# Row-wise dot products with a softmax: who sums step 6, where the last loads of x are cut, and who sets the ones

## The chip, the cores and the metric

The kernel runs on one core of one Trainium2 chip. The metric is the device time of one execution in microseconds; a lower number is better. The times shown are medians of several executions, and beside them stands one execution that was profiled: its instructions and DMA packets come from the trace.

## The reference

```
def reference(x, y):                      # x, y: 8 x 4096 x 512, float32
    gram = np.matmul(x, y.transpose(0, 2, 1))
    diag = np.diagonal(gram, axis1=1, axis2=2)
    diag = diag - diag.max(axis=-1, keepdims=True)
    exp = np.exp(diag)
    return (exp / exp.sum(axis=-1, keepdims=True)).astype(np.float32)
```

Only the diagonal of each product is used, so what must be computed is, for each of 8 x 4096 rows, the dot product of a row of x with the same row of y (512 elements), and then a softmax over the 4096 dot products of each of the 8 batches. Each input is 67 MB and is read once.

## The kernel before

**Layout.** Four batches (Q) stand on the 128 partitions at a time, 32 partitions (G) a batch, so each partition holds 128 rows (C) of one batch. The two halves of the batches make 2 x 128 rows a partition. The work goes in S = 8 steps of R = 32 rows a partition: steps 0 to 3 give the first four batches, 4 to 7 the last four. A step's x is 128 x 16384 floats, 8 MB, and so is its y. x has two buffers (`xs0`, `xs1`, taken by step number modulo 2), y has one (`ys`). The dot products of a half are the columns of `diag0` and `diag1`; step 6 gives columns 64 to 95 of `diag1`, step 7 columns 96 to 127.

**Order.** The schedule is written out by hand: each engine runs its instructions in the order of the program, and an instruction waits only for the data and the buffers that it needs. All loads go out on one queue, SP's, and are worked off in that order.

**Steps 0 to 5** (the first loop of the main part). SP loads 32 rows of x and 32 of y. ScalarE copies the last 6 rows of y aside (`side`), VectorE multiplies x by y in place (`products`, L76), the rows of 26 first and then the 6 from `side`, so that `ys` comes free for the next load before the last product. Then VectorE sums 30 rows with one reduction (`sums`, L79) and ScalarE two rows with one instruction a row (`sums_act`, L84: a copy with an accumulated sum, and an accumulator read). After step 3 the softmax of the first half runs (`exps`, `normalize`).

**Step 6.** The loads are the same. ScalarE copies rows 8 to 16 of y (9 rows) to the unused end of the other x buffer, L146. VectorE multiplies rows 0 to 7, then 8 to 16 from the copy, then 17 to 31. The first of these frees rows 0 to 16 of `ys` for step 7, the last one frees the rest. ScalarE then sums rows 0 to 29, VectorE rows 30 and 31, and VectorE takes the maximum of columns 0 to 63 of `diag1` into a spare column, C + 1 (`largest`, L104).

**Step 7.** GpSimd sets 16 columns behind `ys` to 1 (L156; the program order puts it here, it waits for nothing and runs at the start). SP's loads come in pieces: x in 15, 8, 6, 2 1/2 and 1/2 rows, y in 17, 9, 3 and three times 1. Between the loads the program lists the dot products whose x and y are both in by then. Each row is one VectorE instruction with an accumulated sum (`dot`, L87), shown in the profile as SCALAR_TENSOR_TENSOR and DVE_READ_ACCUMULATOR. When 17 rows are done, VectorE takes the maximum of columns 64 to 111 into column C.

Row 31 is split into two dots, as its x comes in two pieces. The first writes its sum into the column of the x buffer just behind row 31 (`chained`). The second is one column longer than its piece: it takes in that sum, times the 1 that stands behind `ys`. Thus it waits for the last load of x (L182), for the first part's accumulator and for the ones.

**The end.** ScalarE copies columns 0 to 95 of `diag1` (L186). The first half's result is stored by SP in six pieces. Then VectorE takes the maximum over columns 112 to 129, over the partitions of a batch, ScalarE makes the exponentials and their sums, VectorE the sum over the partitions, its reciprocal and the product, and ScalarE's queue stores the last half's result (L191).

The lines that set the cuts, before:

```
    for load, n in (
        (load_x, H - 1), (load_y, F), (load_x, 8), (load_y, 9), (load_x, 6), (load_y, 3), (load_y, 1)
    ):                                   # H = 16, F = 17
        load(t, upto[load], n)
        upto[load] += n
        both = min(upto.values())
        dots(t, done, both - done)
        done = both
```

Of the kernel before, what the change touches and what calls it, by code (L numbers as in the profile page):

```python
# [11 lines left out]
def kernel(  # L12
# [6 lines left out]
    nc = tc.nc  # L19
# [5 lines left out]
    B, N, D = x.shape  # L25
# [3 lines left out]
    C = N // G  # L29
    R = 32  # L30
    H = R // 2
    K = 6
    W = 2
    F = H + 1
    L = 9
    E = 16
    V = D // 2
    S = B // Q * (C // R)


# [9 lines left out]
    yflat = big.tile([P, R * D + E], f32, name="ys")  # L50
# [4 lines left out]
    diag = [small.tile([P, C + 2 * i], f32, name=f"diag{i}") for i in range(B // Q)]  # L55
# [6 lines left out]
    def rows(t, r0, n):  # L62
        return xs[t % 2][:, r0 : r0 + n, :]

    def dots_of(t, r0, n):
        return diag[t * R // C][:, columns(t, r0, n)]
# [4 lines left out]
    def load_y(t, r0, n):  # L71
        nc.sync.dma_start(out=ys[:, r0 : r0 + n, :], in_=yv[t * R // C, :, columns(t, r0, n), :])

    def products(t, r0, n, yt):
        xt = rows(t, r0, n)
        nc.vector.tensor_tensor(out=xt, in0=xt, in1=yt, op=Alu.mult)  # L76

    def sums(t, r0, n):
        nc.vector.tensor_reduce(out=dots_of(t, r0, n), in_=rows(t, r0, n), axis=X, op=Alu.add)  # L79

    def sums_act(t, r0, n):
        for r in range(r0, r0 + n):
            row = xs[t % 2][:, r, :]
            nc.scalar.activation(out=row, in_=row, func=Act.Copy, accum_out=dots_of(t, r, 1))  # L84

    def dot(xt, yt, out):
        nc.vector.scalar_tensor_tensor(  # L87
            out=xt, in0=xt, scalar=1.0, in1=yt, op0=Alu.mult, op1=Alu.mult, accum_out=out
        )

    def dots(t, r0, n):
        for r in range(r0, r0 + n):
            dot(xs[t % 2][:, r, :], ys[:, r, :], dots_of(t, r, 1))

    def over_quadrant(name, column, op, negate=False):

        got = small.tile([P, 1], f32, name=name)
        nc.vector.tensor_reduce(  # L98
            out=got, in_=column.to_broadcast([P, G]), axis=X, op=op, negate=negate, apply_transpose=True
        )  # L100
        return got

    def largest(out, d):
        nc.vector.tensor_reduce(out=out, in_=d, axis=X, op=Alu.max)  # L104

    def exps(i, d):
        mxp = small.tile([P, 1], f32, name=f"mxp{i}")
        largest(mxp, d)
        nmx = over_quadrant(f"nmx{i}", mxp, Alu.max, negate=True)
        sump = small.tile([P, 1], f32, name=f"sump{i}")  # L110
        nc.scalar.activation(out=res[i], in_=diag[i][:, :C], func=Act.Exp, bias=nmx, scale=1.0, accum_out=sump)  # L111
        return sump

    def normalize(i, sump):
        total = over_quadrant(f"sum{i}", sump, Alu.add)
        rc = small.tile([P, 1], f32, name=f"rc{i}")
        nc.vector.reciprocal(out=rc, in_=total)  # L117
        nc.vector.tensor_single_scalar(out=res[i], in_=res[i], scalar=rc, op=Alu.mult)  # L118
# [4 lines left out]
    nc.vector.addr_align(128, offset=0, max_nops=0)  # L123
    nc.scalar.addr_align(128, offset=0, max_nops=0)

    nc.sync.drain()
    nc.sync.drain()

# [13 lines left out]
    t = S - 2  # L142
# [4 lines left out]
    products(t, 0, F - L, ys[:, : F - L, :])  # L147
    products(t, F - L, L, spare)
    products(t, F, R - F, ys[:, F:, :])
    sums(t, R - W, W)  # L150
    sums_act(t, 0, R - W)
    largest(diag[1][:, C + 1 :], diag[1][:, : C - 2 * R])


    t += 1
    nc.gpsimd.memset(yflat[:, R * D :], 1.0)  # L156
    chained = xflat[t % 2][:, R * D : R * D + 1]
    late = R * D - V
    upto = {load_x: 0, load_y: 0}
    done = 0  # L160
    for load, n in (
        (load_x, H - 1), (load_y, F), (load_x, 8), (load_y, 9), (load_x, 6), (load_y, 3), (load_y, 1)
    ):
        load(t, upto[load], n)
        upto[load] += n
        both = min(upto.values())
        dots(t, done, both - done)
        done = both
        if done == F:
            largest(diag[1][:, C : C + 1], diag[1][:, C - 2 * R : C - R + H])  # L170

    first = (R - 3) * D
    xt = xflat[t % 2]
    xrow = xv[t * R // C].rearrange("p c d -> p (c d)")
    end = ((t % (C // R)) + 1) * R * D
    nc.sync.dma_start(out=xt[:, first : late], in_=xrow[:, end - R * D + first : end - V])
    dots(t, done, 1)
    load_y(t, R - 2, 1)
    dots(t, R - 2, 1)
    load_y(t, R - 1, 1)  # L180
    dot(xt[:, late - V : late], yflat[:, late - V : late], chained)
    nc.sync.dma_start(out=xt[:, late : R * D], in_=xrow[:, end - V : end])  # L182
    dot(xt[:, late : R * D + 1], yflat[:, late : R * D + 1], dots_of(t, R - 1, 1))

# [2 lines left out]

    for p, n in ((0, H), (H, H), (2 * H, H), (3 * H, H), (4 * H, 2 * H), (6 * H, 2 * H)):
        nc.sync.dma_start(out=ov[0, p : p + n, :], in_=res[0][p : p + n, :])
    normalize(1, exps(1, diag[1][:, C - R + H :]))  # L190
    nc.scalar.dma_start(out=ov[1], in_=res[1])  # L191


# [28 lines left out]
```

## Time and profile before

| | |
|---|---|
| median of 3 runs | 319.77 us (319.74 to 320.01) |
| profiled execution | 319.84 us |
| its span, first to last instruction | 318.1 us |
| VectorE busy | 241.6 us, 76% of the span, 100 instructions |
| ScalarE busy | 49.8 us, 16%, 97 instructions |
| GpSimd busy | 0.3 us, 5 instructions |
| read from HBM | 134.22 MB, 422 GB/s over the span |
| VectorE's products (L76) | 96.7 us in 8 instructions of the long form, 20.1 in 6 of the short one |
| VectorE's sums (L79) | 98.1 us in 7 instructions |
| VectorE's dots of step 7 (L87) | 20.0 us in 33 instructions |
| ScalarE's sums (L84) | 25.9 us in 42 instructions |

How to read it: DVE in the profile is VectorE, ACT is ScalarE, POOL is GpSimd, SP is SyncE, which only issues DMAs here. A "q" behind an engine's name is its sequencer. The span is counted from the first instruction, and all times in the timeline are us from there. L87 is line 87 of the kernel, and where a helper records an operation, it is the helper's line. In the timeline the columns are the start, the length, the engine, the line, the operation, out<-in with shapes, and in brackets the idle time before it with what ended that. A line of the DMA issues has the size of the load in KB and the us from its issue to its landing.

### The profile page before, as it was taken

How to read it: one execution, taken by the hardware profiler on the slowest of the kernel's cores; microseconds unless marked ns; L12 is line 12 of the kernel's file. 1: busy time of each engine (PE TensorE's matmuls, PEld its weight loads, DVE VectorE, ACT ScalarE, POOL GpSimd, SP SyncE). 2: the span in 40 equal slices, each digit the busy share in tenths (PEclk: the TensorE clock that was granted, in tenths of full speed). 3: DMA queues.
4: the chain of work that ended last, by engine and by line, in shares of the span. 5: the costliest groups of instructions: out<-in, count | busy, mean ns of one | idle time of the engine just before them, and what ended most of it. 6: DMA issues, size and time to landing. Idle time of an engine off the chain costs nothing. (4 is left out here: it accounts for less than half of the span.)

```text
span 318.1 us, 320 instructions
## 1 busy us (share of the span) xinstructions
DVE 241.6 (76%) x100; ACT 49.8 (16%) x97; POOL 0.3 (0%) x5
## 2 busy tenths in 40 slices
DVE  0000069995899939999399994999939998599995
ACT  1000030100301003010020103101030100596700
POOL 0000000000000000000000000000000000000000
DMA  9999999999999999999999999999999999999993
GB/s 373 420 396 478 445 396 437 486 396 396 478 445 396 453 470 396 396 478 445 396 470 453 396 396 486 437 396 478 445 396 404 519 396 396 441 435 399 449 405 129
DMA packets 3971, 134.37 MB, mean 422 GB/s; under 512 B 513, under 2 KB 897, under 8 KB 1537
## 3 DMA queue, kind: packets, MB, share of 16 engines
q1 hardware_dynamic: 3824, 134.29, 97.9%
q10 hardware_dynamic: 144, 0.07, 0.1%
q14 instruction: 3, 0.02, 0.0%
HBM read 134.22 MB, written 0.13 MB: 422 GB/s over the span
## 5 line engine op out<-in xcount | busy, mean ns | idle before, releaser
L76 DVE TENSOR_TENSOR xs<-xs,ys 128x13312 f32<-128x13312 f32 (+2 forms) x8 | 96.7, 12091 | 71.4 <-DMA ys<-in_y_dram 71.4
L79 DVE TENSOR_REDUCE diag<-xs 128x30 f32<-128x15360 f32 (+1 forms) x7 | 98.1, 14020 | 0.2
L84 ACT ACTIVATE xs<-xs 128x512 f32<-128x512 f32 x42 | 25.9, 616 | 90.4 <-DVE xs L76 90.4
L132 ACT ACTIVATE side<-ys 128x3072 f32<-128x3072 f32 x6 | 16.6, 2763 | 124.0 <-DMA ys<-in_y_dram 124.0
L87 DVE SCALAR_TENSOR_TENSOR xs<-xs,ys 128x512 f32<-128x512 f32 (+2 forms) x33 | 20.0, 673 | 0.8 <-DMA ys<-in_y_dram 0.6
L76 DVE TENSOR_TENSOR xs<-xs,side 128x3072 f32<-128x3072 f32 x6 | 20.1, 3351 | 0.0
L84 ACT ACTIVATION_READ_ACCUMULATOR xs<-xs 128x1 f32 x42 | 7.8, 186 | 0.0
L146 ACT ACTIVATE xs<-ys 128x4608 f32<-128x4608 f32 x1 | 4.0, 4043 | 20.0 <-DMA ys<-in_y_dram 20.0
L111 ACT ACTIVATE res<-diag,nmx 128x128 f32<-128x128 f32 x2 | 0.8, 401 | 29.9 <-DVE nmx L98 29.9
L76 DVE TENSOR_TENSOR xs<-xs,xs 128x4608 f32<-128x4608 f32 x1 | 5.0, 4951 | 0.0
L87 DVE DVE_READ_ACCUMULATOR xs<-xs,ys 128x1 f32 x33 | 2.8, 84 | 0.0
L122 ACT ACT_TABLE_LOAD x1 | 1.3, 1283 | 0.7 <-PEq L206 0.7
L98 DVE TRANSPOSE_TENSOR_REDUCE sum<-sump 128x1 f32<-128x32 f32 x2 | 0.4, 211 | 1.2 <-ACT res L111 1.2
L118 DVE TENSOR_SCALAR res<-res,rc 128x128 f32<-128x128 f32 x2 | 0.6, 286 | 0.1
L104 DVE TENSOR_REDUCE mxp<-diag 128x1 f32<-128x128 f32 (+1 forms) x2 | 0.5, 229 | 0.1
L98 DVE TRANSPOSE_TENSOR_REDUCE nmx<-mxp 128x1 f32<-128x32 f32 x2 | 0.4, 212 | 0.1
L104 DVE TENSOR_REDUCE diag<-diag 128x1 f32<-128x64 f32 (+1 forms) x2 | 0.4, 204 | 0.0
L117 DVE RECIPROCAL rc<-sum 128x1 f32<-128x1 f32 x2 | 0.3, 164 | 0.1
L111 ACT ACTIVATION_READ_ACCUMULATOR res<-diag,nmx 128x1 f32 x2 | 0.4, 186 | 0.0
L186 ACT ACTIVATE met<-diag 128x96 f32<-128x96 f32 x1 | 0.3, 283 | 0.0
L156 POOL MEMSET ys<- 128x16 f32 x1 | 0.1, 111 | 0.3 <-POOLq L206 0.3
L206 POOL MEMSET const-bfloat16-1.0<- 128x1 bf16 x1 | 0.1, 101 | 0.0
(3 smaller groups left out, 0.3 us busy)
## 6 DMA issues: line engine op xcount, KB each, us to landing
ys<-in_y_dram SPq DMA_DIRECT2D x1, 4352.0 KB, 14.8
xs<-in_x_dram SPq DMA_DIRECT2D x1, 3840.0 KB, 14.2
ys<-in_y_dram SPq DMA_DIRECT2D x1, 2304.0 KB, 12.2
xs<-in_x_dram SPq DMA_DIRECT2D x1, 2048.0 KB, 19.3
xs<-in_x_dram SPq DMA_DIRECT2D x1, 1536.0 KB, 15.6
ys<-in_y_dram SPq DMA_DIRECT2D x1, 768.0 KB, 16.9
ys<-in_y_dram SPq DMA_DIRECT2D x3, 256.0 KB, 18.3
xs<-in_x_dram SPq DMA_DIRECT2D x1, 640.0 KB, 18.2
```

The costliest lines, as they stand in the source:

```text
L76: nc.vector.tensor_tensor(out=xt, in0=xt, in1=yt, op=Alu.mult)
L79: nc.vector.tensor_reduce(out=dots_of(t, r0, n), in_=rows(t, r0, n), axis=X, op=Alu.add)
L84: nc.scalar.activation(out=row, in_=row, func=Act.Copy, accum_out=dots_of(t, r, 1))
L87: nc.vector.scalar_tensor_tensor(out=xt, in0=xt, scalar=1.0, in1=yt, op0=Alu.mult, op1=Alu.mult, accum_out=out)
L98: nc.vector.tensor_reduce(out=got, in_=column.to_broadcast([P, G]), axis=X, op=op, negate=negate, apply_transpose=True)
L104: nc.vector.tensor_reduce(out=out, in_=d, axis=X, op=Alu.max)
L111: nc.scalar.activation(out=res[i], in_=diag[i][:, :C], func=Act.Exp, bias=nmx, scale=1.0, accum_out=sump)
L117: nc.vector.reciprocal(out=rc, in_=total)
L118: nc.vector.tensor_single_scalar(out=res[i], in_=res[i], scalar=rc, op=Alu.mult)
L122: nc.scalar.preload_act_table(Act.Exp)
L132: nc.scalar.activation(out=side, in_=ys[:, R - K :, :], func=Act.Copy)
L146: nc.scalar.activation(out=spare, in_=ys[:, F - L : F, :], func=Act.Copy)
```

## The change

- Step 6: ScalarE sums all 32 rows. VectorE's sum of rows 30 and 31 and its maximum of columns 0 to 63 go.
- Step 7: x comes in 12, 11, 6, 2 3/8 and 5/8 rows in place of 15, 8, 6, 2 1/2 and 1/2. Row 31 is cut after 192 columns in place of 256 and its second part has 320. The loads of y and the order of all loads stay.
- The maximum behind row 16 of step 7 now spans columns 0 to 111 in place of 64 to 111. The last maximum spans columns 112 to 128 (17 values) in place of 112 to 129.
- The ones: VectorE sets one column ahead of step 0, in place of GpSimd's 16 columns.

```diff
-    V = D // 2
+    V = 5 * D // 8
+    U = D - V
...
+    nc.vector.memset(yflat[:, R * D : R * D + 1], 1.0)
+
     nc.sync.drain()
     nc.sync.drain()
...
-    sums(t, R - W, W)
-    sums_act(t, 0, R - W)
-    largest(diag[1][:, C + 1 :], diag[1][:, : C - 2 * R])
+    sums_act(t, 0, R)
...
-    nc.gpsimd.memset(yflat[:, R * D :], 1.0)
...
-        (load_x, H - 1), (load_y, F), (load_x, 8), (load_y, 9), (load_x, 6), (load_y, 3), (load_y, 1)
+        (load_x, R - L - 11), (load_y, F), (load_x, 11), (load_y, 9), (load_x, 6), (load_y, 3), (load_y, 1)
...
-            largest(diag[1][:, C : C + 1], diag[1][:, C - 2 * R : C - R + H])
+            largest(diag[1][:, C : C + 1], diag[1][:, : C - R + H])
...
-    dot(xt[:, late - V : late], yflat[:, late - V : late], chained)
+    dot(xt[:, late - U : late], yflat[:, late - U : late], chained)
...
-    normalize(1, exps(1, diag[1][:, C - R + H :]))
+    normalize(1, exps(1, diag[1][:, C - R + H : C + 1]))
```

## The prediction

> **What bounds the kernel now.** I read the page first, then SP's timeline with the landing times of its loads, then VectorE's timeline of the last step, each for what ends last.
>
> ```profile
> DVE 241.6 (76%) x100; ACT 49.8 (16%) x97; POOL 0.3 (0%) x5
> ...
> DMA  9999999999999999999999999999999999999993
> ...
> HBM read 134.22 MB, written 0.13 MB: 422 GB/s over the span
> ```
>
> The reader is to see that no engine is full, but that the 16 DMA engines are, in every slice but the last. All of the input passes once through them. So the first question about any edit is whether it moves the moment at which the last byte lands.
>
> SP's timeline of the last loads (start, length, engine, line), and then the size and the time from issue to landing of five of them, from the DMA view:
>
> ```profile
> 269.10 0.33 SPq L69 DMA_DIRECT2D xs<-in_x_dram  x1
> 278.74 0.33 SPq L72 DMA_DIRECT2D ys<-in_y_dram  x1
> 279.12 0.43 SPq L69 DMA_DIRECT2D xs<-in_x_dram  x1
> 291.64 0.33 SPq L72 DMA_DIRECT2D ys<-in_y_dram  x1
> ...
> 293.44 0.43 SPq L176 DMA_DIRECT2D xs<-in_x_dram  x1
> ...
> 298.46 0.33 SPq L182 DMA_DIRECT2D xs<-in_x_dram  x1
> ```
>
> ```profile
> ys<-in_y_dram SPq DMA_DIRECT2D x1, 4352.0 KB, 14.8
> xs<-in_x_dram SPq DMA_DIRECT2D x1, 3840.0 KB, 14.2
> ...
> xs<-in_x_dram SPq DMA_DIRECT2D x1, 2048.0 KB, 19.3
> ...
> xs<-in_x_dram SPq DMA_DIRECT2D x1, 640.0 KB, 18.2
> xs<-in_x_dram SPq DMA_DIRECT2D x1, 128.0 KB, 14.7
> ```
>
> Issue plus landing time gives the order in which data comes in: x rows 0 to 14 at 283.3, y rows 0 to 16 at 293.5, x rows 15 to 22 at 298.4, and at the end x row 29 to half of row 31 at 311.6 and the last half row at 313.2. Eight rows of 256 KB take 298.4 - 293.5 = 4.9 us, so a row takes 0.61 us, in one unbroken line: each load is issued 3 us or more before the one ahead of it is through. The last byte lands at 313.2.
>
> VectorE beside it:
>
> ```profile
> 291.65 1.22 DVE L79 TENSOR_REDUCE diag<-xs 128x2 f32<-128x1024 f32 x1
> 292.79 0.21 DVE L104 TENSOR_REDUCE diag<-diag 128x1 f32<-128x64 f32 x1
> 293.63 0.69 DVE L87 SCALAR_TENSOR_TENSOR xs<-xs,ys 128x512 f32<-128x512 f32 x1 [0.64 <-DMA ys<-in_y_dram]
> ...
> 311.70 0.69 DVE L87 SCALAR_TENSOR_TENSOR xs<-xs,ys 128x512 f32<-128x512 f32 x1
> ...
> 312.93 0.42 DVE L87 SCALAR_TENSOR_TENSOR xs<-xs,ys 128x256 f32<-128x256 f32 x1
> 313.27 0.08 DVE L87 DVE_READ_ACCUMULATOR xs<-xs,ys 128x1 f32 x1
> 313.45 0.43 DVE L87 SCALAR_TENSOR_TENSOR xs<-xs,ys 128x257 f32<-128x257 f32 x1
> ```
>
> From 293.63 on it works without a pause: 32 rows, one each 0.61 us. It reaches row 29 at about 311.6, just when that row's x lands (311.6), so in the last 2 us VectorE and the loads are level. Only the last dot is behind its data: x is there at 313.2, it starts at 313.45. Behind it comes a fixed tail (largest, exp, sum, division, store) of 318.1 - 313.45 = 4.6 us.
>
> **The sums of step 6.** Off VectorE go the sum of two rows (1.22 us at 291.65) and the maximum over 64 (0.21 at 292.79), some 1.3 us in all, ahead of the first dot. They do not set that dot: it waits a further 0.64 us for y, which lands at 293.5. Taken alone this edit is worth nothing at the end. ScalarE gets two more rows at 0.61 us (its own pitch: 298.40, 299.01). It now does 15 rows from 291.65 on instead of 13, so it ends near 300.9 instead of 299.6; its next need is the exp at 314.4, which leaves 13 us of cover. The moved maximum grows from 48 to 112 columns (0.20 us for 48, 0.21 for 64: I take 0.2) and gets a new wait on ScalarE's last sum. Queued behind it on VectorE are all dots from row 17 on. It is reached at 302.3 (below), 1.4 us after ScalarE is through, so the wait costs nothing; were ScalarE later, a further 1.6 us of waiting for y would still cover it.
>
> **The cut of x.** The first x load falls from 15 rows to 12, so the y load behind it lands 3 x 0.61 = 1.8 us earlier, at 291.7, with VectorE free at 291.65. Rows 0 to 11 then run from 291.8 to 299.2. The next 11 x rows land at the old 298.4, since as many bytes are ahead of their end (40 rows before and after). Rows 12 to 16 run to 302.2, the maximum to 302.3. Then VectorE must wait for the next y load, issued at 291.64 as before, because it waits for the last product of step 6, which this change does not touch; it takes 12.2 us on the page, so it lands at 303.8. That is 1.5 us of new idle time: the gained start is given back there. From there the loads lead: x rows 23 to 28 land at 307.6 (292.01 + 15.6), the next y at 309.4 (292.49 + 16.9), and rows 26 to 28 end at 311.3, before x row 29 comes.
>
> **The last two pieces.** The larger one loses 64 columns (32 KB, 0.08 us), so it lands near 311.55 and row 29 starts at 311.62; rows 30 and 31 follow each 0.61 later, row 31's first part at 312.85, with their y 0.08 us earlier too. A dot of 512 columns takes 0.61 to its accumulator read and one of 256 takes 0.34 (312.93 to 313.27), so a column costs 1.05 ns and 192 columns take 0.27: accumulator read at 313.12. The last dot needs that value; the old distance from read to start is 0.18, giving 313.30. Its x lands at the old 313.2, since the total of bytes ahead is the same, and 0.09 us from landing to start (293.54 to 293.63) gives 313.25 to 313.29. I take 313.30, 0.15 earlier than now. It is then 64 columns longer: 0.07. Net **-0.08 us**. The maximum of 17 in place of 18 values and the rest of the tail stay.
>
> **The ones.** GpSimd's set (0.11 us at 0.73) goes and VectorE sets one column at about 0.8 us, where it is idle for 42 us until step 0's data lands; no load touches that column. If that cover were gone it would cost about the 0.1 of GpSimd's row. The last dot then has one engine less to wait for, which could shorten its 0.18 us by at most the 0.09 that lies between the end of the accumulator read and the dot's start; the landing at 313.2 lets it keep none to 0.05 of it. I take 0.
>
> **Sum.** The profiled execution is 319.84 (span 318.1 and 1.7 around it), so 319.84 - 0.08 = 319.76; it lies 0.07 above the median of 319.77, so the median becomes 319.69: **319.7 us**. A difference under 0.2% (0.64 us) is what a measurement here can't tell from none, so this is no change.
>
> **The price that this trace does not show: the start of the y load.** The y load at 278.74 can only go out once step 6's first product is done. Today x ahead of it covers its start. The DMA view, in slices of 25 ns from 281.9:
>
> ```profile
> DMA  0000000909909009900009000000000090999000
> ...
> DMA packets 32, 0.56 MB, mean 557 GB/s; under 512 B 16, under 2 KB 16, under 8 KB 16
> ```
>
> These are the 16 engines' first packets of y, at 282.1 to 282.8, 3.3 to 4.1 us after issue. With three x rows less the engines are free at 280.2 to 281.0, 1.5 to 2.2 us after issue. How long an issued load needs to start is shown once: the first load of the program goes out at 0.83, and its packets start at 1.85 to 2.85, 1.0 to 2.0 us later. If the same engine is last both times, nothing is lost; in the opposite order an engine would lose 2.0 - 1.5 = 0.5 us. From above the loss is bounded by the cover that has been enough so far, 3.3 us: at most 3.3 - 1.5 = 1.8. From below by 0, since an earlier start of y is already counted. I take 0, by the start row, the nearest.
>
> The Trainium skill, DMA: Bandwidth & Descriptors, section "Latency and other measured facts", puts the first byte of a load issued by SP at about 0.6 us; by that the cover would be ample and the sum would stay as it is. This trace does not agree: its one uncovered start took 1.0 to 2.0 us, so the risk stays.
>
> **Rivals.** (1) Slower: the y load starts too late, as just worked out. It decides from a start of 1.5 us on, and every tenth goes to the end one for one, because all later loads stand in the same line and the tail hangs on the last. Price 0.1 to 1.8, time 319.8 to 321.5; over the 0.2% only from a start of some 2.2 us on. For it: the uncovered start comes within 0.5 us of that. Against it: that start was the program's first. (2) Faster: VectorE's work, not the loads, sets the end, and 1.8 us of earlier start come through, or most of them: 318.0 to 318.5. For it: 20 us without a pause. Against it: the last x lands at 313.2, and 4.9 us of dot and tail follow; starting with its data, the dot can gain 0.2 at most. It needs loads that end earlier too, as from 302 to 313.2 they run at 391 GB/s against 432 from 23 to 302; at the full rate 11.2 us would be 10.1, so 1.1 us faster, 318.7. Nothing in the change raises that rate. (3) The sums don't fit: ScalarE is slower beside VectorE's dots than its 0.61 and the maximum waits. It needs 3 us of delay to be felt; before, ScalarE held its pitch beside the dots.
>
> **Chances.** Forecast, with a small start loss included: 0.83. Rival 1 above 0.2%: 0.09. Rival 2: 0.06. Rival 3: 0.02, half of it past 0.2%. So faster 0.06, same 0.84, slower 0.10. The range takes the forecast with the spread of the runs before (319.74 to 320.01), a gain of 0.3 more and the 0.5 us of a late start: 319.3 to 320.2.
>
> **What would show it.** Right: first dot at about 291.8, an idle gap of about 1.5 us on VectorE waiting for y after row 16, row 29 waiting for x near 311.55, last x landed at 313.2, last dot at 313.3. The late start would show as 16 first packets of y later than 280.2 to 281.0, with every later landing late by as much. VectorE as the bound would show as an end of the chain near 312 with x landed earlier. ScalarE's last sum past 303.9 would prove the third rival.

## The result and the profile after

The changed kernel takes 320.27 us (median of 22 executions, 319.85 to 322.26), the kernel before, on the same chip, 319.96 (22 executions, 319.74 to 320.61). The ratio is 1.0023, 95% interval 1.0012 to 1.0034: slower by a quarter of a percent, where no change was forecast, and the median lies 0.07 us above the forecast range.

The median tells less than the list. Eleven of the 22 executions lie between 319.85 and 320.08, two at 320.47 and 320.66, nine between 321.33 and 322.26, and between 320.66 and 321.33 there is none. So the kernel has two outcomes: in half of the executions it is in the forecast range, with two more a little above it, and in about four of ten it is 1.4 to 2.3 us slower than the kernel before. The profiled execution (322.26, span 320.3) is one of the latter, the slowest of all, which is of use: it shows the loss.

Some 0.15 us of the 0.31 between the medians have nothing to do with the two groups. The time of an execution less its span, the part before the first and after the last instruction, is 1.94 us in the median of the changed kernel (1.87 to 2.03) and 1.79 in the 29 executions of the kernel before that were run beside the first experiments (1.73 to 1.82).

SP's timeline of the last loads, then the same loads in the DMA view (KB, us from issue to landing):

```profile
269.65 0.33 SPq L70 DMA_DIRECT2D xs<-in_x_dram  x1
279.24 0.33 SPq L73 DMA_DIRECT2D ys<-in_y_dram  x1
279.62 0.43 SPq L70 DMA_DIRECT2D xs<-in_x_dram  x1
292.14 0.33 SPq L73 DMA_DIRECT2D ys<-in_y_dram  x1
...
300.71 0.33 SPq L182 DMA_DIRECT2D xs<-in_x_dram  x1
```

```profile
ys<-in_y_dram SPq DMA_DIRECT2D x1, 4352.0 KB, 14.7
xs<-in_x_dram SPq DMA_DIRECT2D x1, 3072.0 KB, 12.3
xs<-in_x_dram SPq DMA_DIRECT2D x1, 2816.0 KB, 21.1
...
xs<-in_x_dram SPq DMA_DIRECT2D x1, 160.0 KB, 14.8
```

Everything in this execution is 0.5 us late from the start of step 7 on (the issue at 269.65 against 269.10); that grew in the steps before, which the change hardly touches, and executions of both kernels differ by that much. Add issue and landing time (the second view has the time to the tenth, the landing records give 281.96 and 293.97): 12 rows of x are in at 282.0, y's 17 rows at 294.0. Between these two landings lie 12.0 us; before, for the same 4352 KB, it was 293.54 - 283.28 = 10.26. So **1.75 us are lost in the one load of y**, and nothing after it brings them back: the last x lands at 315.5, 2.3 later than before.

VectorE beside it:

```profile
294.10 0.69 DVE L88 SCALAR_TENSOR_TENSOR xs<-xs,ys 128x512 f32<-128x512 f32 x1 [1.98 <-DMA ys<-in_y_dram]
...
304.51 0.27 DVE L105 TENSOR_REDUCE diag<-diag 128x1 f32<-128x112 f32 x1
306.15 0.69 DVE L88 SCALAR_TENSOR_TENSOR xs<-xs,ys 128x512 f32<-128x512 f32 x1 [1.37 <-DMA ys<-in_y_dram]
...
313.87 0.69 DVE L88 SCALAR_TENSOR_TENSOR xs<-xs,ys 128x512 f32<-128x512 f32 x1 [0.24 <-DMA xs<-in_x_dram]
...
315.58 0.49 DVE L88 SCALAR_TENSOR_TENSOR xs<-xs,ys 128x321 f32<-128x321 f32 x1
```

VectorE now waits three times, each time for a load: it has lost its sums, and it is the loads alone that set the end. The last dot starts 0.09 us after its x has landed (300.71 + 14.8 = 315.5).

Where in y's load the time goes can be seen in the DMA view with a narrow window. The digits are the busy share in 40 slices, placed by the start of each packet; packets under 512 B are the 16 engines' closing writes of the x load, the others first packets of y. First the changed kernel from 280.85 to 282.2, then, for the same 1.35 us from the first such write on, the kernel of the first experiment (15 rows of x ahead, from 281.95):

```profile
DMA  0909990009900900090900900000000000009000
...
DMA packets 31, 0.52 MB, mean 387 GB/s; under 512 B 16, under 2 KB 16, under 8 KB 16
```

```profile
DMA  0099990099900900900099900000900000000000
...
DMA packets 32, 0.56 MB, mean 413 GB/s; under 512 B 16, under 2 KB 16, under 8 KB 16
```

Of 32 packets one is missing in the changed kernel, and one stands alone in slice 37: fourteen engines start y at once, one starts at 282.1, and one still hasn't at 282.2. In the trace's packet records these two start 0.5 and 1.0 us behind the last of the others, at 282.08 and 282.58, though by the packet records both had been through with x since 281.1. Their first packet of 34 KB takes 2.40 and 2.06 us; of the other fourteen, eight take 1.29 and six 1.33 to 1.61. The landings follow: the 16 engines' parts of y's load are in from 291.6 to 294.0, a spread of 2.3 us; before it was 0.8. The trace does not name the engines, but in y's load and in each of the nine loads of x and y behind it two parts of 16 land 1.2 us behind the rest.

The Trainium skill, DMA: Bandwidth & Descriptors, section "Why a DMA increments its semaphore by 16 and not by 1", says that the engines of one DMA finish independently and that only the full count of 16 means that all data are there. The trace agrees: two engines of 16 set the landing of the whole load at 294.0, while half of them had landed by 292.1.

### The profile page after: what moved, and what is told of

It is laid out like the page before. It is cut to its first block, busy times and chain, and to the rows that moved or that the text cites. A ratio compares the mean times of both kernels' runs of the same rounds, so it can differ in the third digit from the quotient of the medians.

```text
span 320.3 us, 321 instructions
## 1 busy us (share of the span) xinstructions
DVE 240.6 (75%) x99; ACT 51.0 (16%) x101; POOL 0.2 (0%) x4
## 4 chain that ended last, share of the span: by engine, by line
DMA 70%; DVE 28%; issue 0%; SPq 0%; ACT 0%; DVEq 0%
DMA ys<-in_y_dram 59%; DVE xs L77 28%; DMA xs<-in_x_dram 11%; DVE xs L88 0%; SPq L73 0%; SPq L70 0%; DVE res L119 0%; DVE sum L99 0%; DVE nmx L99 0%; ACT res L112 0%; DVE mxp L105 0%; DVE rc L118 0%; DVEq L77 0%; DVEq L88 0%; SPq L130 0%
## 5 line engine op out<-in xcount | busy, mean ns | idle before, releaser
L80 DVE TENSOR_REDUCE diag<-xs 128x30 f32<-128x15360 f32 x6 | 96.9, 16153 | 0.2
L85 ACT ACTIVATE xs<-xs 128x512 f32<-128x512 f32 x44 | 27.1, 617 | 90.4 <-DVE xs L77 90.4
```

## The experiments

Theory A: with 12 rows of x ahead of it, y's load is issued too short a time before the DMA engines are free. Single engines begin it late or slowly and lag to the end, which the parts of the later loads bear out. Its rivals: another part of the change (theory B), the load of 12 rows itself, or the load that is issued 0.4 us behind y (A2, against A1, the start of y's own load). The experiments were run on three chips, each beside the kernel before on the same chip.

**The first cut back to 15 and 8 rows, all else changed.**

```diff
-        (load_x, R - L - 11), (load_y, F), (load_x, 11), (load_y, 9), ...
+        (load_x, H - 1), (load_y, F), (load_x, 8), (load_y, 9), ...
```

> The changed kernel with x's first two loads back at 15 and 8 rows; all else of the change stays. Theory A (step 7's first y load starts too late behind 12 rows of x, and single DMA engines then lag to the end): no execution above 320.7, median 319.6 to 320.0, y of 17 rows landing 10.2 to 10.4 us after the x ahead of it. Theory B (the 192 + 320 cut of row 31, the sums on ScalarE or the ones are to blame): part of the executions stay at 321.3 or more, as in the changed kernel.

Measured: 320.01 (11 executions, 319.81 to 320.40), ratio to the kernel before 1.0003 (0.9995 to 1.0012). The upper group is gone, and y's load takes 10.26 us again. The sums on ScalarE, the cut of row 31 and the ones bring nothing that can be measured. They, or one of them, do cost a little outside the span: it is 1.92 us here (1.88 to 2.01), and 1.79 before.

**The first cut alone, in the kernel before.**

```diff
-        (load_x, H - 1), (load_y, F), (load_x, 8), (load_y, 9), ...
+        (load_x, 12), (load_y, F), (load_x, 11), (load_y, 9), ...
```

> The kernel before with only x's first two loads changed to 12 and 11 rows. Theory A: two groups of executions, near 319.9 and 1.4 to 2 us above, at 321.3 to 322.3, some four in ten of them in the upper one. Theory B: all between 319.7 and 320.6 as before.

Measured: 321.02 (12 executions, 319.79 to 322.65), ratio 1.0035 (1.0020 to 1.0050); six of the 12 at 321.19 or more. So the cut alone makes the loss. Two clear groups were expected; here the values in between (320.5 to 320.9) are filled too. In its profile y's load takes 11.6 us. Outside the span it has 1.78 us, as before.

**13 rows, 14 rows, 8 rows** (the changed kernel with 13 and 10, 14 and 9, 8 and 15).

> The changed kernel with 13 and 10 rows. Theory A: 0.6 us more cover for the y load, 2.1 us from its issue to the first free engine; the upper group gets rarer or is gone, median 319.7 to 320.1. Theory B: as the changed kernel, some four executions in ten at 321.3 or more.

> The changed kernel with 14 and 9 rows. Theory A: cover 2.7 us, the upper executions nearly gone, median 319.8 to 320.2, highest below 320.8. With the medians of 15, 13, 12 and 8 rows (320.0, 320.6, 320.3 or 321.0, 322.6) this gives the cost against the cover.

> The changed kernel with 8 and 15 rows: the DMA engines have no x left some 0.2 to 0.9 us before the y load is even issued, so the y load starts from idle queues and its first packets show the bare time from issue to start. Theory A: first packets 1.0 to 2.4 us after issue, every landing behind it later by 2 to 3 us, every execution at 321.8 to 324. Theory B: as the changed kernel, 319.9 or 321.5.

Measured: 13 rows 320.58 (11 executions, 319.83 to 321.26, ratio 1.0020, 1.0010 to 1.0029); 14 rows 320.37 (319.88 to 320.82, 1.0005, 0.9996 to 1.0014); 8 rows 322.56 (322.38 to 322.61, 1.0082, 1.0069 to 1.0095). With more cover the highest values come down: 322.3, 321.3, 320.8, 320.4 for 12, 13, 14 and 15 rows. The last step of these says little: the 320.82 of 14 rows is the profiled execution, in which y's load takes 10.26 us, as before, and step 6's y lands 0.79 us late. The medians were expected 0.5 (13 rows) and 0.2 (14 rows) lower than they are, and that of 13 rows is above that of 12 (320.27).

The kernel with 8 rows shows a bare start. Its y load is issued at 279.14, after the engines have run out of x. The DMA view from 278 to 281, 75 ns a slice:

```profile
DMA  0000500000000000000000000000999009900909
...
DMA packets 32, 0.57 MB, mean 191 GB/s; under 512 B 15, under 2 KB 15, under 8 KB 15
```

By the packet records 15 of the 16 engines are through with x by 278.6 and the last at 279.0, and nothing starts until 280.1. The first packets of y start 1.0 to 1.8 us after issue, and each of these 16 takes 1.62 to 2.16 us, where the next ones take 1.29. So here a start from nothing costs two things, the wait for the first packet and then 0.3 to 0.9 us of slow first packet; together the load of y takes 12.5 us from landing to landing and not 10.26.

**The same bytes ahead, in loads of 12 and 3 rows.**

```diff
-        (load_x, R - L - 11), (load_y, F), (load_x, 11), (load_y, 9), ...
+        (load_x, 12), (load_x, 3), (load_y, F), (load_x, 8), (load_y, 9), ...
```

> The changed kernel, but the 15 rows of x that stood ahead of y before are back as two loads, 12 and 3 rows, and then y's 17 and x's 8. The load of 12 rows stays, the bytes ahead of y are those of before. Theory A (cover of the y load's start by bytes): all executions between 319.7 and 320.5, as with 15 rows in one load. Rival (it is the load of 12 rows itself, its packets or the count of loads): an upper group at 321.2 or more stays.

Measured: 320.10 (11 executions, 319.89 to 320.69), ratio 1.0007 (0.9998 to 1.0016). Nothing above 320.7, though four executions are above the 320.5 that was expected (the kernel before goes to 320.4 on this chip); y's load takes 10.26 us. It is not the load of 12 rows, it is what lies ahead of y in the queue.

**y issued later, the loads of x untouched.** The kernel before, with 6 rows copied by ScalarE in step 6 and not 9, so that VectorE's first product is 11 rows long.

```diff
-    L = 9
+    L = 6
```

> The kernel before, its loads of x untouched (15 and 8 rows), but ScalarE's copy in step 6 is 6 rows and not 9, so that VectorE's first product is 11 rows and the y load goes out 1.7 us later, near 280.4. Theory A: the cover falls from 3.3 to 1.7 us, between the kernels with 12 and 13 rows; an upper group appears though no load was changed, median 320.4 to 321. Rival (the cut of x): all at 319.7 to 320.4, as before.

Measured: 321.52 (5 executions, 321.16 to 322.08), ratio 1.0047 (1.0034 to 1.0060). Its SP timeline and its two loads of interest:

```profile
269.29 0.33 SPq L69 DMA_DIRECT2D xs<-in_x_dram  x1
280.50 0.33 SPq L72 DMA_DIRECT2D ys<-in_y_dram  x1
```

```profile
ys<-in_y_dram SPq DMA_DIRECT2D x1, 4352.0 KB, 15.2
xs<-in_x_dram SPq DMA_DIRECT2D x1, 3840.0 KB, 14.3
```

x lands at 283.55 and y at 295.72 by the landing records, 12.2 us apart, with no load changed: the loss goes with the time at which y is issued. Two first packets of y take 2.39 and 2.93 us; the engine of the one starts on time, that of the other late. The loss is larger than expected. The engines reach y 2.1 us after its issue here, as with 13 rows, where the highest execution was at 321.26 and the lowest at 319.83, while here the lowest is at 321.16. So the cover in us is not all that counts.

**y issued earlier, the cut kept.** In the first form the first y load has 13 rows, with shorter first products in step 6, and the second y load has 13 rows too. The two maxima are cut at row 13 to match, which the diff leaves out.

```diff
-    F = H + 1
-    L = 9
+    F = 13
+    L = 7
...
-        (load_x, R - L - 11), (load_y, F), (load_x, 11), (load_y, 9), ...
+        (load_x, 12), (load_y, F), (load_x, 11), (load_y, 26 - F), ...
```

> The changed kernel with x in 12 and 11 rows, but the first y load is 13 rows and not 17 and ScalarE's copy in step 6 is 7 rows and not 9, so that this load can go out 1.1 us earlier (near 277.6); the second y load is 13 rows, and the two maxima are cut at row 13 of step 7. Theory A: cover from issue to the first free engine 2.6 us, between the kernels with 13 and 14 rows; hardly an execution above 320.7, median 319.8 to 320.2. Rival (the 12 rows themselves): as the changed kernel, some four in ten at 321.2 or more.

Measured: 322.64 (5 executions, 322.44 to 323.13), ratio 1.0080 (1.0067 to 1.0093). The time tells nothing of the start, as the edit brings in another bound: VectorE has four rows more to do behind the second y load, and works from 304.54 to the end without a pause, so that its last dot starts at 315.97 though its x is there at 313.9. The profile tells something: with y reached 2.7 us after its issue, the 13 rows take 8.38 us, 0.5 more than the same rows in the second form (7.86), and two first packets take 1.20 and 1.67 us where the others take 0.99. The second form keeps VectorE's rows: y in 13 and 4 rows, the 4 freed by a second copy of ScalarE.

```diff
-    nc.scalar.activation(out=spare, in_=ys[:, F - L : F, :], func=Act.Copy)
-    products(t, 0, F - L, ys[:, : F - L, :])
-    products(t, F - L, L, spare)
+    A, M = 6, 7
+    nc.scalar.activation(out=spare[:, :M, :], in_=ys[:, A : A + M, :], func=Act.Copy)
+    nc.scalar.activation(out=side[:, : F - A - M, :], in_=ys[:, A + M : F, :], func=Act.Copy)
+    products(t, 0, A, ys[:, :A, :])
+    products(t, A, M, spare[:, :M, :])
+    products(t, A + M, F - A - M, side[:, : F - A - M, :])
...
-        (load_x, R - L - 11), (load_y, F), (load_x, 11), ...
+        (load_x, R - L - 11), (load_y, A + M), (load_y, F - A - M), (load_x, 11), ...
```

> The changed kernel with x in 12 and 11 rows, y's first load in two: 13 rows that can go out near 277.7, 1.1 us earlier, as step 6's first product is 6 rows and ScalarE's copy 7, and 4 rows that go out near 279.3 behind them, freed by a second copy of ScalarE. VectorE has the same rows to do after each landing as in the changed kernel. Theory A: cover 2.6 us for the first of them; no execution above 320.8, median 319.9 to 320.4. Rival (the 12 rows themselves): some four in ten at 321.2 or more.

Measured: 320.60 (11 executions, 320.15 to 321.12), ratio 1.0018 (1.0010 to 1.0027). SP's timeline and the first y load in the DMA view:

```profile
269.74 0.33 SPq L70 DMA_DIRECT2D xs<-in_x_dram  x1
278.28 1.91 SPq L73 DMA_DIRECT2D ys<-in_y_dram  x2
280.24 0.42 SPq L70 DMA_DIRECT2D xs<-in_x_dram  x1
```

```profile
ys<-in_y_dram SPq DMA_DIRECT2D x1, 3328.0 KB, 11.6
```

No execution is above 321.2, so the upper group is gone with the cut of 12 rows kept, and in its profile all first packets of y are on time, 2.8 us after issue (0.99 us each but for one of 1.05). But the median is 0.2 us above what was expected and the highest 0.3. Hardly any of that time lies in the loads of step 7. In all executions 2.07 to 2.16 us lie outside the span, 0.35 more in the median than in the kernel before; in the profiled one, step 6's y lands 0.6 us late as well. What lengthens the part outside the span stays open.

**The next load held back**, once with 12 rows ahead and once with 8: a copy of one element by ScalarE, into a row of the next load of x, keeps that load from going out until 283.75 (283.99 with 8 rows). The edit, and SP's timeline with 12 rows:

```diff
-    sums_act(t, 0, R)
+    sums_act(t, 0, 8)
+    nc.scalar.activation(out=rows(t + 1, 12, 1)[:, 0, :1], in_=side[:, 0, :1], func=Act.Copy)
+    sums_act(t, 8, R - 8)
```

```profile
278.64 0.33 SPq L73 DMA_DIRECT2D ys<-in_y_dram  x1
283.75 0.33 SPq L70 DMA_DIRECT2D xs<-in_x_dram  x1
```

> The changed kernel (12 and 11 rows), but the load of 11 rows, issued 0.4 us behind the y load so far, is held back to some 283.7 by one small ScalarE copy into its first row, so that the y load starts alone. Theory A1 (the y load's own start is what needs the cover): as the changed kernel, some four executions in ten at 321.2 or more, single first packets of y of 2 us or more. Theory A2 (the start of the next load, 0.4 us behind, disturbs single engines just when they begin y): no execution above 320.7, all first packets of y at 1.3 us.

> The kernel with 8 and 15 rows, the load of 15 held back to some 283.7 in the same way. Theory A1: its 16 first packets of y still take 1.6 to 2.2 us each, where later ones take 1.29; time near 322.5. Theory A2: the first packets take 1.3 us and the time falls by some 0.5 us, to 321.9 to 322.1.

Measured: 321.75 (12 executions, 319.96 to 323.11, ratio 1.0050, 1.0032 to 1.0069) and 322.58 (322.42 to 322.94, 1.0081, 1.0069 to 1.0094). A2 falls: with y starting alone, eight of 12 are at 321.4 or more, and two first packets take 2.29 and 2.41 us. With 8 rows ahead, the time is that of the kernel without the hold, but the packets are not all as expected: the eight that start first, up to 1.4 us after issue, take 1.7 to 2.1 us, the other eight, up to 2.2 us after issue, 1.29 to 1.47. The load of y takes 12.6 us all the same.

**The account.** Take for each profiled execution the loss in y's load (landing of y less landing of the x ahead, less 10.26), how late step 6's y landed against the 274.16 of before, and how much more time lies outside the span than the 1.78 of before. The first two are from the trace's landing records. The two kernels with y's first load in 13 rows are left out, as another load can't be held against 10.26.

| kernel | first packet of y after its issue | loss in y's load | step 6's y late by | outside the span, over 1.78 | 319.84 + all three | measured |
|---|---|---|---|---|---|---|
| changed, 12 and 3 rows | 3.6 | 0.00 | -0.18 | 0.14 | 319.80 | 319.89 |
| changed, 15 rows | 3.2 | 0.01 | 0.09 | 0.14 | 320.08 | 319.99 |
| changed, 14 rows | 2.6 | 0.00 | 0.79 | 0.23 | 320.86 | 320.82 |
| changed, 13 rows | 2.1 | 0.20 | -0.04 | 0.23 | 320.23 | 320.21 |
| before, 15 rows, y later | 2.1 | 1.91 | 0.16 | 0.00 | 321.91 | 322.03 |
| changed (12) | 1.7 | 1.75 | 0.50 | 0.23 | 322.32 | 322.26 |
| before with 12 rows | 1.5 | 1.31 | -0.01 | -0.01 | 321.13 | 321.19 |
| 12 rows, next load held | 1.6 | 1.58 | -0.10 | 0.33 | 321.65 | 321.60 |
| changed, 8 rows | 1.0 | 2.23 | 0.40 | 0.14 | 322.61 | 322.54 |
| 8 rows, next load held | 1.0 | 2.31 | 0.15 | 0.32 | 322.62 | 322.58 |

The three columns give each measured time to within 0.12 us, so in these executions nothing else of any size is at work.

## Why the prediction was wrong

**What bounds the kernel**: right. The landing of the last byte sets the end in all of these kernels but one (the first with y in 13 rows), and what delays one load delays the end by as much.

**The sums of step 6**: right in effect. VectorE's 1.3 us came off a stretch in which it then waited (1.98 us for y). The larger maximum takes 0.27 us, not 0.2; it followed the dot ahead of it without a wait for ScalarE. The forecast wait of 1.5 us behind it measured 1.37, after a late start.

**The last two pieces and the ones**: right as far as it can be seen. In the kernel with 15 rows and the rest of the change the last dot starts at 313.40, 0.09 late by step 6, so at 313.31 on the clock of before, where 313.30 was worked out; it is 0.42 us to its accumulator read, 0.07 more than before, as forecast. The net -0.08 is too small for the executions to tell (1.0003, 0.9995 to 1.0012).

**The 1.7 us around the span**: the sum took them over unchanged. They grew by some 0.15 us in the changed kernel, by 0.13 with the first cut taken back, but not in the two kernels that differ from the one before in a cut or a copy alone (1.78 and 1.80). So it is some other part of the change; which, and why, stays open.

**The cut of x**: this step failed, in the term priced at nothing, the start of the y load. Nine of 22 executions lost 1.4 to 2.3 us, the profiled one 1.75 in this load. The prediction named the place and the mechanism, as its first rival, and gave it 0.09. It went wrong in two ways. It read one number, 1.0 to 2.0 us from issue to the first packet, as the whole price of a start, and so took 0.5 us as the loss to reckon with inside the range; the late engines here started 2.8 and 3.3 us after issue, and first packets can be slow as well, 2.40 and 2.06 us here and 1.62 to 2.16 in the bare start with 8 rows, for 1.29. And it took the start to be the same in each execution, and late for all 16 engines if it was late. It is not: the same kernel loses next to nothing in six executions of ten and 1.4 to 2.3 us in four, and in the profile it is two engines of 16 that are late. The rule "if the same engine is last both times, nothing is lost" was a guess about engines, and the range went to 320.2 on it. The bound from above, 1.8 us for a cover of 1.5, came near the 1.75 by luck: by the same rule a cover of 2.1 bounds the loss by 1.2, and with y issued later 1.91 were lost.

That the median came out beyond the range, by 0.07 us, is in part chance. The kernel before came out 0.19 above the 319.77 that the forecast started from, and the time outside the span added some 0.15; without either the median would lie in the range, and four executions in ten would still be slower.

What stays open: why single engines begin y late although it was issued 1.5 to 2.1 us ahead. The late ones of the changed kernel start 2.8 and 3.3 us after issue, while all 16 of the bare start with 8 rows had begun at 1.8. The next load's issue is excluded. Why 2.1 us cost little with 13 rows and 1.2 us or more each time with y issued later is not explained either; the two were run on different chips, and each has one profile.

No kernel here beats the one before. The cut of x gives VectorE slack that the end, set by the loads, can't use; with the cut taken back, the rest of the change is level with before.

## What to carry to other kernels

In a kernel bound by its loads, look at how long before its turn each load is issued: that cover is a resource, and cutting the load ahead spends it. A row that shows a start once gives neither its spread over 16 engines and many executions nor the slow first packet; when the cover falls as it did here, from 3.3 us to 1.5, count on a loss in part of the executions, and test it by moving the issue and the bytes ahead one at a time. And look at the list of executions ahead of the median: two groups hint at something that happens in only part of them.

## What the runs showed of the hardware that was not expected

A load that started on idle queues had its first packets 1.0 to 1.8 us after issue, and these took 1.62 to 2.16 us for 34 KB that otherwise take 1.29; in a second such kernel they started 1.0 to 2.2 us after issue, and only the earlier half of them was slow (1.7 to 2.1).

Where the engines were still busy with the load ahead, most began the next one within some 10 ns of their last write, and in four of these profiles one or two of 16 began late, up to 3.3 us after issue. In the changed kernel the two late parts stayed 1.2 us behind the rest through nine later loads of x and y (the parts of the last x landed from 313.3 to 315.5).
